# Four of the scan stage's output weight sums added by the DMA engines in place of GpSimd

## The chip, the cores and the metric

The kernel runs on one core of a Trainium2 chip. The metric is the device time in microseconds (us) of one execution; a kernel's time is the median of several runs. A profile is one further execution, recorded by the hardware profiler. Its span runs from the first to the last instruction, and its own device time is a little longer than the span.

## The reference

One layer of a diffusion backbone, in float32, over 1024 latent tokens of width 1024 and 256 context tokens ahead of them. The token mixer is a two-directional S5 state-space scan: 64 groups of 16 channels with 64 complex states each. A SwiGLU feed-forward block with 2816 hidden units follows.

```python
def s5_direction(u_ctx, u_lat, lam_re, lam_im, log_step, b_re, b_im, c_re, c_im):
    lam_bar = jnp.exp(lam * jnp.exp(log_step)[:, None])
    b_bar = ((lam_bar - 1.0) / lam)[..., None] * lax.complex(b_re, b_im)
    c_mat = lax.complex(c_re, c_im)
    def run(u, h0):
        bu = jnp.einsum('lgh,gnh->lgn', u, b_bar)
        bu = bu.at[0].add(lam_bar * h0)
        a = jnp.broadcast_to(lam_bar, bu.shape)
        _, h = lax.associative_scan(_linear_combine, (a, bu), axis=0)
        return jnp.einsum('lgn,ghn->lgh', h, c_mat).real, h[-1]
    ...
# around it: rms_norm, modulate, gelu and a gated product (GLU), then
# x + gate * swiglu(...), and a last rms_norm
```

The sums that the change touches belong to the last line of `run`: the output weights C times powers of lam_bar, one table for each of the eight token positions inside a chunk. They are complex products, so each entry is the sum of two real products.

## The kernel before

The tokens are cut into chunks of eight. A chunk's input goes into states by one set of matmuls; VectorE then runs the recurrence over the chunks, 159 of them with the context; and each chunk's outputs come from the state before it, times the output weight tables, plus a within-chunk product that acts on the inputs directly. The 64 groups are handled as four quarters q, each with two directions d. A quarter's table `CL[q]` has four parts, part = 2 ri + d (real or imaginary, forward or backward), each 128 x 1024 floats.

The order of the whole stage is written out by hand in `PROG1` (L32) and `PROG2`: a list of steps, each a letter and a number, which `run` (L945) walks through. All engines get their instructions in that order, each engine its own. The steps that matter here:

- **Cqp** (C22 is quarter 2, part 2): `cl_ops` (L660). GpSimd makes one product into the table (`prod(0, o)`), a second into a scratch tile (`prod(1, ct)`), and the two are added. The string `HOWS` (L30) has a letter for each of the sixteen sums that tells who adds: P is TensorE, E is GpSimd, Y is a transfer with accumulation that GpSimd's queue issues (L676). The first two sums of quarter 0 are issued ahead of the program with Y already, as are twelve others of an earlier stage (L434). The scratch tiles are given out by `cts` (L696): C22, C31 and C33 share one (in region `rw`), C30 and C32 another (in region `ra`).
- **Kn** (K4 and K5 are quarter 2, K6 and K7 quarter 3): `k_mats` (L806) multiplies the tables on TensorE for the within-chunk product (matmuls L813, L817, L821); ScalarE copies the result out (L825) and stores it to memory (L826).
- **Tn**: `toeplitz` (L828). SyncE loads from that memory (`ra<-kd`, L834) what the within-chunk matmul of a half quarter needs.
- **Rk**: `turned(k, 0)` (L899). ScalarE copies the backward states of half quarter k in reversed order (L906); it needs VectorE's scan of that half quarter.
- **Pk, Xk, Sk, pk**: TensorE's output matmuls of half quarter k for the first half of the chunks; `x_mm` (L936) is the within-chunk part, `states_mm` (L926) the part from states. P4 needs T8 and T9. P6 and P7 are written p6 and p7, since their `x_mm` comes in `PROG2`.
- **Yn**: ScalarE copies the result out of the accumulation banks (L988). f7 is a small piece of the scan that GpSimd does.

The end of `PROG1` reads `C22 C23 R2 X2 K4 K5 S2 Y4 Y5 R3 P3 Y6 Y7 T8 T9 T10 T11 C30 C31 R4 P4 Y8 Y9 C32 C33 f7 M2 m0 R5 P5 Y10 Y11 R6 p6 Y12 Y13 R7 K6 p7 Y14 Y15 K7 T12 ... T15`. VectorE has the scan as its own long list, which runs beside all of it; `PROG2` then does the second half of the chunks (N0 to N7), GELU and the start of the GLU.

```python
            def add():
                if how is PE:
                    ...
                elif how is SY:
                    E.dma_start(o, ct, accum_op=ADD)
                else:
                    tt(o, o, ct, ADD, E)

            o = CL[q][:, ri, d]
            return [lambda: prod(0, o), lambda: prod(1, ct), add]
...
        HOW = [[{"P": PE, "Y": SY, "E": E, "V": V}[c] for c in h] for h in HOWS.split()]
```

Of the kernel before, what the change touches and what calls it, by code (L numbers as in the profile page):

```python
# [26 lines left out]
NS = 64  # L27
EPS = 1e-6
MAGIC = 12582912.0
HOWS = "PPPP PPEE PEEE EEEE"  # L30
ZEN = "VVSVSVSV"
PROG1 = ("A22 B0 A26 C02 G1 A30 A34 C03 A40 K0 A44 A48 C10 K1 L2 A54 G2 C11 A60 F10 C12 F11 C13 T0 T1 T2 T3 A64 M0 M1 K2 K3 R0 P0 Y0 Y1 L3 R1 C20 P1 Y2 Y3 T4 "  # L32
         "T5 G3 T6 T7 C21 C22 C23 R2 X2 K4 K5 S2 Y4 Y5 R3 P3 Y6 Y7 T8 T9 T10 T11 C30 C31 R4 P4 Y8 Y9 C32 C33 f7 M2 m0 R5 P5 Y10 Y11 R6 p6 Y12 Y13 R7 K6 p7 Y14 Y15 K7 T12 T13 T14 T15")
# [10 lines left out]
def s5_ffn_kernel(tc, a, out):  # L44
# [3 lines left out]
    with ctx:  # L48
# [1040 lines left out]

        HOW = [[{"P": PE, "Y": SY, "E": E, "V": V}[c] for c in h] for h in HOWS.split()]  # L1090
        run(PROG1)
# [667 lines left out]
```

## Time and profile before

| | |
|---|---|
| median of 3 runs | 1015.07 us (1015.01 to 1017.59) |
| the profiled execution, its own time | 1015.25 us |
| its span | 1013.0 us |
| TensorE busy | 959.5 us, 95% |
| GpSimd busy | 752.3 us, 74% |
| VectorE busy | 781.8 us, 77% |

The scan stage lies at about 130 to 235 us of the span, and the steps from C22 to K7 at 182 to 231 us. In rows of the timeline, "idle before" in square brackets is the time in which that engine stood still ahead of the instruction, and behind the arrow stands what ended it. PE is TensorE's matmuls, PEld its weight loads, DVE VectorE, ACT ScalarE, POOL GpSimd, SP SyncE; a q behind a name is that engine's instruction queue. "issue" means that the profile shows nothing that was waited for.

### The profile page before, as it was taken

The numbers are of one execution on the slowest core, as the hardware profiler recorded it, in microseconds if no ns is written. First come the engines' busy times: TensorE is split into PE (matmuls) and PEld (weight loads), VectorE is DVE, ScalarE is ACT, GpSimd is POOL, SyncE is SP. The second block draws the span as 40 slices with busy tenths as digits, with TensorE's granted clock in tenths as the row PEclk, the third lists the DMA queues.
The fourth block names the chain that finished last, engine by engine and source line by source line (L and its number), as shares of the span: only waits on it lengthen the run. The fifth ranks groups of instructions, "written<-read, shape, count | busy, mean of one in ns | idle before, by whom it ended". The sixth has DMA issues, their size and how long they took to land. (4 is left out here: it accounts for less than half of the span.)

```text
span 1013.0 us, 18603 instructions
## 1 busy us (share of the span) xinstructions
PE 959.5 (95%) x6988; PEld 770.5 (76%) x6988; DVE 781.8 (77%) x1694; ACT 441.7 (44%) x862; POOL 752.3 (74%) x574
## 2 busy tenths in 40 slices
PE   5988797878999999999999999999999999999996
PEld 1466423777999988778888888888888888888885
DVE  7979799995456867877958677686958677686987
ACT  5478622335544663443343343324343343424337
POOL 5799898980872448979785878777786877777674
PEclk9999999999999999999999999999999999999998
DMA  9765996324512021011212111121212111121205
GB/s 335 280 137 97 315 332 235 93 72 142 188 47 80 1 104 63 27 44 46 73 42 83 42 52 42 49 66 52 74 42 83 43 49 46 43 72 53 73 21 166
DMA packets 48545, 98.95 MB, mean 98 GB/s; under 512 B 4284, under 2 KB 18876, under 8 KB 47176
## 3 DMA queue, kind: packets, MB, share of 16 engines
q1 hardware_dynamic: 43272, 86.64, 25.9%
q0 software_dynamic: 2016, 7.34, 3.8%
q10 hardware_dynamic: 3168, 3.79, 1.1%
q8 instruction: 55, 0.90, 0.4%
q14 instruction: 34, 0.28, 0.1%
HBM read 84.25 MB, written 6.17 MB: 89 GB/s over the span
## 5 line engine op out<-in xcount | busy, mean ns | idle before, releaser
L78 POOL TENSOR_TENSOR c<-rxc,c 128x512 fp32r<-128x512 f32 x128 | 166.6, 1316 | 53.2 <-ACT c L1213 52.4
L1273 PE MATMUL ut<-ra,c 128*128 128x512 f32 x400 | 155.7, 389 | 1.2 <-DVE ra L78 1.2
L1272 PE MATMUL ut<-ra,c 128*128 128x512 f32 x400 | 155.7, 389 | 0.2 <-ACT ra L1213 0.2
L1274 PE MATMUL ut<-ra,c 128*128 128x512 f32 x400 | 155.6, 389 | 0.0
L1213 ACT CAST c<-rxc 128x512 fp32r<-128x512 f32 x128 | 79.0, 622 | 146.5 <-PE xt L1567 53.0
L1567 PE MATMUL xt<-c,c 128*128 128x512 f32 x540 | 129.7, 389 | 0.0
L78 DVE TENSOR_TENSOR ru<-ru,xt 128x1024 f32<-128x1024 f32 x90 | 107.8, 1216 | 13.4 <-PE xt L1567 9.4
L1567 PEld LDWEIGHTS xt<-c,c 128*128 128x128 f32 x540 | 101.4, 188 | 21.0
L78 DVE TENSOR_TENSOR ru<-ut,ru 128x512 f32<-128x512 f32 x98 | 67.2, 686 | 43.0 <-PE ut L1274 37.6
L1273 PEld LDWEIGHTS ut<-ra,c 128*128 128x128 f32 x400 | 75.1, 188 | 17.1 <-POOL rxc L78 1.5
L1272 PEld LDWEIGHTS ut<-ra,c 128*128 128x128 f32 x400 | 75.1, 188 | 16.1 <-ACT ra L1213 0.6
L1274 PEld LDWEIGHTS ut<-ra,c 128*128 128x128 f32 x400 | 75.1, 188 | 15.5
L78 POOL TENSOR_TENSOR c<-rw,c 128x512 fp32r<-128x512 f32 (+1 forms) x29 | 39.8, 1372 | 37.7 <-ACT c L1213 37.7
L78 POOL TENSOR_TENSOR c<-ru,c 128x512 fp32r<-128x512 f32 (+1 forms) x39 | 58.8, 1508 | 10.1 <-ACT c L1213 5.7
L1272 PE MATMUL ut<-c,c 128*128 128x512 f32 x160 | 62.3, 390 | 0.8 <-DVE rxa L78 0.8
L78 POOL TENSOR_TENSOR rxc<-rxc 128x512 f32<-128x512 f32 x40 | 61.5, 1537 | 1.6
L1273 PE MATMUL ut<-c,c 128*128 128x512 f32 x160 | 62.3, 389 | 0.0
L1274 PE MATMUL ut<-c,c 128*128 128x512 f32 x160 | 62.2, 389 | 0.0
L1567 PE MATMUL ut<-c,c 128*128 128x512 f32 x216 | 51.9, 389 | 0.0
L78 DVE TENSOR_TENSOR pe<-pe,ru 128x256 f32<-128x256 f32 x64 | 27.4, 428 | 29.3 <-ACT pe L1113 16.2
L585 PE MATMUL pv<-ru,c 128*64 128x160 f32 x512 | 44.4, 313 | 5.7 <-ACT rxa L389 1.8
L78 DVE TENSOR_TENSOR ru<-ru,ut 128x512 f32<-128x512 f32 x76 | 47.2, 679 | 0.3
(439 smaller groups left out, 2569.5 us busy)
## 6 DMA issues: line engine op xcount, KB each, us to landing
c<-in_ada_w SPq DMA_DIRECT2D x46, 256.0 KB
rxc<-in_w SPq DMA_DIRECT2D x38, 256.0 KB
rxc<-in_w SPq DMA_DIRECT2D x19, 512.0 KB
ru<-in_w SPq DMA_DIRECT2D x11, 512.0 KB
rw<-in_w SPq DMA_DIRECT2D x11, 512.0 KB
ra<-in_ada_w SPq DMA_DIRECT2D x10, 512.0 KB
ra<-in_ada_w SPq DMA_DIRECT2D x18, 256.0 KB
ru<-in_xT SPq DMA_DIRECT2D x4, 1024.0 KB
```

What stands on the lines that cost most here:

```text
L78: eng.tensor_tensor(out=o, in0=x, in1=y, op=op)
L585: PE.matmul(pv[64 * (i % 2):64 * (i % 2) + 64, ri, c0:c0 + 160], w[:, i, 64 * ri:64 * ri + 64], U[:, 8 * b + 4 * j + i], start=True, stop= ...
L1213: S.copy(o[0], x)
L1272: PE.matmul(pu, wh, bh, start=start, stop=False)
L1273: PE.matmul(pu, wh, bl, start=False, stop=False)
L1274: PE.matmul(pu, wl, bh, start=False, stop=stop)
L1567: PE.matmul(pd, w[:, cs_], b, start=j in (1, 2, 4) and n == 0, stop=n == 2, skip_group_check=j not in (1, 2, 4))
```

## The change

Four letters of `HOWS` go from E to Y: C22, C30, C31 and C32. The sums C23 and C33 stay with GpSimd, C20 with TensorE.

```diff
-HOWS = "PPPP PPEE PEEE EEEE"
+HOWS = "PPPP PPEE PEYE YYYE"
```

On GpSimd, four tensor additions become four transfers that its queue issues. Here is its list from C30's second product on, to C33's (`c_66` is the table of quarter 3, `ra` and `rw` hold the scratch tiles, `rxc` and `rxa` the factors):

```order
 L78 TENSOR_TENSOR ra<-rxc,rxa 128x1024 [waits DMAHW5_49,DMAHW3_49,Activation_49]
-L78 TENSOR_TENSOR c_66<-c_66,ra 128x1024 [waits Pool_49]
+L676 DMA c_66<-ra 128x1024 [waits Pool_49]
 L78 TENSOR_TENSOR c_66<-rxc,rxa 128x1024
-L78 TENSOR_TENSOR rw<-rxc,rxa 128x1024
-L78 TENSOR_TENSOR c_66<-c_66,rw 128x1024 [waits Pool_49]
+L78 TENSOR_TENSOR rw<-rxc,rxa 128x1024 [waits DMASW6_49]
+L676 DMA c_66<-rw 128x1024 [waits Pool_49]
 L78 TENSOR_TENSOR c_66<-rxc,rxa 128x1024
-L78 TENSOR_TENSOR ra<-rxc,rxa 128x1024
-L78 TENSOR_TENSOR c_66<-c_66,ra 128x1024 [waits Pool_49]
+L78 TENSOR_TENSOR ra<-rxc,rxa 128x1024 [waits DMASW7_49]
```

Each addition has become a transfer in the same place, and a product that fills a scratch tile anew now waits for the transfer that read it: C31's for C22's (DMASW6), C32's for C30's (DMASW7), and likewise C33's for C31's.

On TensorE nothing moves; only waits change. In p6, the first consumer of quarter 3's table:

```order
-L926 MATMUL pw<-c_66,ra 64x128 [waits DVE_49,PE_49,Pool_49]
+L926 MATMUL pw<-c_66,ra 64x128 [waits DMASW7_49,DVE_49,PE_49]
 L926 MATMUL pw<-c_66,ra 64x128 [waits Activation_49]
-L926 MATMUL pw<-c_66,ra 64x128 [waits Activation_49,Pool_49]
+L926 MATMUL pw<-c_66,ra 64x128 [waits DMASW0_49,Activation_49]
 L926 MATMUL pw<-c_66,ra 64x128
-L926 MATMUL pw<-c_66,ra 64x128 [waits Pool_49]
+L926 MATMUL pw<-c_66,ra 64x128 [waits DMASW1_49]
 L926 MATMUL pw<-c_66,ra 64x128
 L926 MATMUL pw<-c_66,ra 64x128 [waits Pool_49]
```

The parts C30, C31 and C32 are waited for through the transfers' semaphores; the last row, for C33, still waits for GpSimd. In K4 the first matmul that reads C22 waits for its transfer, where before it had only the wait for C23, two groups of eight matmuls ahead of it:

```order
 L813 MATMUL kt<-c_65,rxa 16x112
 L813 MATMUL pm<-c_65,rxa 16x112
-L813 MATMUL kt<-c_65,rxa 16x112
+L813 MATMUL kt<-c_65,rxa 16x112 [waits DMASW6_49]
 L813 MATMUL pm<-c_65,rxa 16x112
 L813 MATMUL kt<-c_65,rxa 16x112
```

No instruction changes its place on VectorE, ScalarE or SyncE.

## Rows read from the trace of the kernel before

**Rows 1.** The page, 40 equal slices of the span: TensorE's busy tenths.
```profile
PE   5988797878999999999999999999999999999996
```
**Rows 2.** Busy time by stretch: PE, PEld, DVE, ACT, POOL, clock, DMA share, GB/s.
```profile
205.00:210.00 5.00, 2.72 (x60) 2.37 (x54) 5.00 (x30) 1.59 (x3) 4.92 (x4) 1.00 0.59 130
```
**Rows 3.** GpSimd's timeline, 120 to 260 us: start, us, engine, line, operation.
```profile
125.98 2.02 POOL L78 TENSOR_TENSOR rw<-rxc,rxa 128x1024 f32<-128x1024 f32 x1 [1.77 <-DMA c<-rw]
128.31 0.88 POOL L676 DMA_DIRECT2D c<-rw  x1 [0.30 <-POOL rw L78]
128.92 10.22 POOL L78 TENSOR_TENSOR c<-rxc,rxa 128x1024 f32<-128x1024 f32 x5
...
159.46 1.40 POOL L78 TENSOR_TENSOR c<-ra,r 128x256 f32<-128x256 f32 x2 [2.31 <-DVE ra L78]
...
183.89 2.02 POOL L78 TENSOR_TENSOR rw<-rxc,rxa 128x1024 f32<-128x1024 f32 x1
185.99 2.36 POOL L78 TENSOR_TENSOR c<-c,rw 128x1024 f32<-128x1024 f32 x1
188.30 4.03 POOL L78 TENSOR_TENSOR c<-rxc,rxa 128x1024 f32<-128x1024 f32 x2
192.41 2.35 POOL L78 TENSOR_TENSOR c<-c,c 128x1024 f32<-128x1024 f32 x1
...
218.18 2.36 POOL L78 TENSOR_TENSOR c<-c,rw 128x1024 f32<-128x1024 f32 x1
```
**Rows 4.** Accumulating transfers of L434 (twelve), then L676 (two), from issue to landing.
```profile
DMA to landing us min/median/max: 4.5/5.5/7.8
...
DMA to landing us min/median/max: 6.1/7.5/8.8
```
**Rows 5.** TensorE's timeline in K4: C23's group, and the first matmul that reads C22.
```profile
194.82 0.27 PE L813 MATMUL kt<-c,rxa 64*16 64x112 f32 x1 [1.53 <-POOL c L78]
...
195.21 0.26 PE L813 MATMUL kt<-c,rxa 64*16 64x112 f32 x1
```
**Rows 6.** TensorE's weight loads in p6.
```profile
219.90 0.36 PEld L926 LDWEIGHTS pw<-c,ra 64*64 64x64 f32 x8 [0.78 <-issue]
220.59 1.81 PEld L926 LDWEIGHTS pw<-c,ra 64*64 64x64 f32 x52 [0.33 <-POOL c L78]
```
**Rows 7.** ScalarE's timeline: R6 and R7.
```profile
219.16 0.63 ACT L906 COPY ra<-ra 128x512 f32<-128x512 f32 x1
...
224.24 0.62 ACT L906 COPY ra<-ra 128x512 f32<-128x512 f32 x1 [0.54 <-DVE ra L78]
```
**Rows 8.** VectorE's timeline: the last piece that R7 needs, and the copy behind the scan.
```profile
223.95 0.20 DVE L78 TENSOR_TENSOR ra<-ra,lta 128x64 f32<-128x64 f32 x1
...
227.30 0.43 DVE L908 COPY ra<-ra 128x512 f32<-128x512 f32 x1
```
**Rows 9.** TensorE's timeline: a stop inside K6, p7's first matmuls, N0's first.
```profile
225.27 0.19 PE L821 MATMUL kt<-rxc,rxa 64*16 64x16 f32 x1 [1.23 <-issue]
...
225.48 0.41 PE L926 MATMUL pw<-c,ra 64*64 64x128 f32 x4
...
230.48 1.22 PE L926 MATMUL pe<-c,ra 64*64 64x128 f32 x28 [0.47 <-ACT rw L825]
```
**Rows 10.** TensorE's timeline: P4's within-chunk matmuls.
```profile
208.15 1.13 PE L936 MATMUL pw<-ra,ru 128*128 128x128 f32 x8 [1.55 <-DMA ra<-kd]
```
**Rows 11.** The page's DMA queues: packets, MB, share of 16 engines' span.
```profile
q0 software_dynamic: 2016, 7.34, 3.8%
```
**Rows 12.** VectorE's timeline: starts of successive scan steps at two places.
```profile
157.31 0.28 DVE L78 TENSOR_TENSOR ltb<-ra,lta 128x128 f32<-128x128 f32 x1
158.37 0.28 DVE L78 TENSOR_TENSOR ltb<-ra,lta 128x128 f32<-128x128 f32 x1
...
193.16 0.28 DVE L78 TENSOR_TENSOR ltb<-ra,lta 128x128 f32<-128x128 f32 x1
194.21 0.28 DVE L78 TENSOR_TENSOR ltb<-ra,lta 128x128 f32<-128x128 f32 x1
```

## The prediction, written before the changed kernel was run

> **What bounds the kernel now.** I read the page's slices first: from slice 10 on, some 250 us, TensorE is busy for nine tenths or more in nearly all of them [rows 1]. A shift of what comes before is carried to the end there, and nothing in that part is touched. The change lies in the scan stage, so I read that stage alone. At 205 to 210 us GpSimd is busy for 4.92 us of 5 and VectorE for all 5, TensorE for 2.72 [rows 2]. VectorE runs the scan without a stop; GpSimd makes the weight tables without a stop; TensorE follows both. So the question is at which places TensorE waits for GpSimd, and what is late next where that wait goes.
>
> In GpSimd's timeline one sum is two products of 2.0 us and an addition of 2.36; C22's addition runs from 185.99, C23's products from 188.30 and its addition from 192.41, and the last addition, C33's, from 218.18 to 220.54 [rows 3].
>
> **What an exchanged sum saves on GpSimd.** With an addition, the next product starts 188.30 - (183.89 + 2.02) = 2.39 us behind the last product's end. With a transfer, which the trace has at 128.31, it starts 128.92 - (125.98 + 2.02) = 0.92 us behind it: the issue occupies 0.88 and the next product overlaps its end [rows 3]. So 1.47 us each, and 5.88 for the four. C23's addition then ends at 194.76 - 1.47 = 193.29. C33's would end at 220.54 - 5.88 = 214.66, less what the new waits cost.
>
> **The new waits on GpSimd.** C32's second product needs C30's transfer to have landed. Between that issue and this product lie a gap of 0.61 us, C31's two products, its issue (0.92 with its gap) and C32's first product: 0.61 + 3 x 1.98 + 0.92 = 7.5 us. The fourteen such transfers of this trace landed 4.5 to 8.8 us after issue, with medians of 5.5 and 7.5 [rows 4]; one of them made the product behind it wait for 1.77 us [rows 3]. So the wait is 0 to 1.3 us, and the same again at C33: C33's addition ends between 214.7 and 217.3. What is queued behind it on GpSimd is f7 and two small steps, and R7 is the first to need f7. Before, f7 came after 220.5; it is now at least 3 us earlier, so these waits cost nothing.
>
> **First place, K4: up to 1.47 us.** TensorE stood still for 1.53 us until C23's addition had ended, and started at 194.82 [rows 5]. That becomes 193.35. The next wait is C22's transfer. It is issued at 183.89 + 2.02 + 0.30 (the gap at 128.31) = 186.2 and lands at 190.7 to 195.0 by the bounds above. It is wanted 0.39 us after the start of C23's group (195.21 against 194.82 [rows 5]), so at 193.74. A landing of 5.5 or 7.5 us is in time; at 8.8 the gain shrinks to 195.21 - 195.0 = 0.2. I take the full 1.47, since both medians lie within the 7.5 us that are there, and keep 0.2 as the other end.
>
> K5, S2 and P3 follow on TensorE without another wait for GpSimd. P4 waits for its table of inputs (1.55 us, until 208.15 [rows 10]), but that table is loaded from what K4 and K5 stored, so it moves with them. R6 thus ends at 219.79 - 1.47 = 218.32 [rows 7].
>
> **Second place, p6: 0.33 us.** p6 began when R6 was there, loaded eight weights and then waited another 0.33 us for C33 [rows 6]. With C33 finished by 217.3 that wait is gone. Together, p6 and K6 can run 1.80 us earlier, and p7 behind them could start at 225.48 - 1.80 = 223.7 [rows 9].
>
> **What is late next: VectorE.** p7 needs R7, and R7 already waited for VectorE: 0.54 us, until the last scan piece of this half quarter at 223.95 + 0.20 [rows 7, 8]. The change moves nothing on VectorE. R7 ends at 224.24 + 0.62 = 224.86; from R6's end at 219.79 to p6's reload at 219.90 it took 0.1 us [rows 6, 7], so p7's backward matmuls start at about 225.0, where they started at 225.5 before. **Of the 1.8 us on offer, 0.5 us is left**; the rest becomes TensorE waiting for R7. Behind p7 come Y14, Y15, K7 and N0 at 230.48 [rows 9]. N0 also needs a copy that VectorE makes behind the scan, done by 227.73 [rows 8]; that is still early for an N0 at 230.0. So the 0.5 us goes on into the part that TensorE fills.
>
> The sum, against the profiled execution's own 1015.25 us (its span 1013.0 and 2.25 around it): 1015.25 - 0.5 = 1014.75. The median of the runs stands 0.18 below that execution, so I predict 1014.6 us.
>
> **Rivals.** (a) *The transfers hold up other transfers: slower.* The four additions move from GpSimd to the DMA engines, just where K4's and K5's results are stored and read back for P4. The fourteen transfers took 3.8% of 16 engines' span [rows 11]: 0.038 x 1013 / 14 = 2.75 us of all engines each. C30's is issued at about 197.6, among K5's stores, and C31's at 202.5, among the loads P4 waits for. The Trainium skill, DMA: Bandwidth & Descriptors, section "Issuing engines are not separate DMA queues", says that transfers started by the scalar, sync or gpsimd engine all end up on the same 16 DMA engines and interleave there. By that rule, what is saved on GpSimd is partly paid by whoever waits for a load. If P4's load is d late, p7 moves by the greater of -0.5 and -1.8 + d, so the point is d = 1.8. One whole transfer ahead of it, d = 2.75: +0.95, 1015.6 to 1016.2. Both, d = 5.5: +3.7, about 1018.8. Against it: in that stretch the engines are busy for 0.59 of the time [rows 2]; 2.75 us more in the 5.5 us of one landing is another 0.50, so 1.09 in all, which delays by 0.09 x 5.5 = 0.5 us, and that hides under the 1.3 us that VectorE's limit leaves.
>
> (b) *C22 lands last, and K4 gains nothing.* The transfer then does not do what it is for. p6's 0.33 us remains: 1014.9 by the profile, 1014.7 by the median. It needs a landing of about 9 us, the worst of fourteen.
>
> (c) *The stop inside K6 stays where it is.* K6 stands still for 1.23 us until 225.27, with no wait that the profile shows [rows 9]. I let it move with K6. If it belongs to the moment and not to K6, p7 still starts at 225.5 and the time stays at 1015.1.
>
> (d) *The scan itself gets faster, and VectorE's limit falls away.* This needs the additions to have slowed VectorE. One scan step took 158.37 - 157.31 = 1.06 us while GpSimd stood idle (its 2.31 us before 159.46 [rows 3]), and 194.21 - 193.16 = 1.05 during C23's addition [rows 12]. So there is nothing to win there; were there, the whole 1.8 would pass: 1013.3. The Trainium skill, SBUF — State Buffer, section "SBUF: two separate sides", states that a VectorE operation with two SBUF inputs contends with a GpSimd operation that reads SBUF. By that rule taken alone each removed addition would free VectorE; the equal steps in the trace speak against it here.
>
> **How the numbers follow.** Forecast 0.55; (a) 0.24, of which 0.08 for more than one transfer's delay; (b) 0.10; (c) 0.05; (d) 0.04; 0.02 for what I have not thought of. The range for 8 in 10 runs from (d), 1013.3, over the forecast, (b) and (c), to (a) with one transfer and something more: 1017.0. About 0.3%, 3 us, is what a measurement of this kernel can tell from no change. None of the cases is faster by that much, (a) with both delays is slower by that much: faster 0.03, same 0.87, slower 0.10.
>
> **What would show it.** Right: no wait for GpSimd at K4 and p6; GpSimd through with C33 by 217.3; R7 waiting for VectorE until the same 224.2, with R6 some 1.3 us earlier; p7 and N0 half a us earlier, and everything behind them by as much. Wrong: K4 waiting for a transfer from `rw` beyond 193.8 (b); P4's wait longer than 1.55 us and R6 later than 219.8 (a); p7 still at 225.5 although p6 ended early (c); scan steps below 1.05 us (d). A difference that arises behind N0 and not before it would be something that none of these steps has.

## The result: slower, by the transfers that wait in front of P4

The changed kernel takes 1018.02 us (median of 12 runs, 1016.38 to 1022.99) against 1014.27 us before (12 runs beside it, 1012.01 to 1017.59). The ratio is 1.0037, 95% interval 1.0026 to 1.0049: slower by 3.75 us. I had forecast 1014.6 us and given slower by over 0.3% a chance of one in ten; the time lies above the range.

What the change does to GpSimd is what I forecast. Its timeline in the changed kernel (start, us, engine, line, operation):

```profile
195.94 2.03 POOL L78 TENSOR_TENSOR ra<-rxc,rxa 128x1024 f32<-128x1024 f32 x1
198.27 0.86 POOL L676 DMA_DIRECT2D c<-ra  x1 [0.30 <-POOL ra L78]
198.88 2.32 POOL L78 TENSOR_TENSOR c<-rxc,rxa 128x1024 f32<-128x1024 f32 x1
200.87 2.31 POOL L78 TENSOR_TENSOR rw<-rxc,rxa 128x1024 f32<-128x1024 f32 x1
203.47 0.88 POOL L676 DMA_DIRECT2D c<-rw  x1 [0.30 <-POOL rw L78]
...
213.67 2.35 POOL L78 TENSOR_TENSOR c<-c,rw 128x1024 f32<-128x1024 f32 x1
```

C30's transfer is issued at 198.27 and C31's at 203.47, 5.20 us apart; a sum with an addition took 192.41 - 185.99 = 6.42 [rows 3]. GpSimd never waits for a transfer between them, and C33's addition ends at 216.02 where it ended at 220.54. TensorE no longer waits for GpSimd at K4 or in p6. The loss comes at P4. TensorE's timeline (idle time before an instruction and what ended it in brackets):

```profile
196.49 0.17 PE L821 MATMUL pm<-rxc,rxa 64*16 64x16 f32 x1 [0.81 <-issue]
199.95 0.17 PE L821 MATMUL pm<-rxc,rxa 64*16 64x16 f32 x1 [1.32 <-issue]
211.26 2.05 PE L936 MATMUL pw<-ra,ru 128*128 128x128 f32 x8 [4.15 <-DMA ra<-kd]
214.04 2.08 PE L936 MATMUL pw<-ra,ru 128*128 128x128 f32 x8 [0.73 <-DMA ra<-kd]
```

P4's second part in the kernel before, next to its first in [rows 10]:

```profile
210.12 1.16 PE L936 MATMUL pw<-ra,ru 128*128 128x128 f32 x8 [0.84 <-DMA ra<-kd]
```

Two things stand there. P4's first wait for its table was 1.55 us [rows 10] and is 4.15; and the same eight matmuls that took 1.13 us [rows 10] take 2.05. The changed kernel by stretch shows what goes with it (us, PE busy, granted clock, DMA share, GB/s):

```profile
206.00:208.00 2.00, 1.11 (x36) 1.00 0.86 136
208.00:210.00 2.00, 0.00 (x0) 1.00 0.62 151
210.00:212.00 2.00, 0.74 (x3) 0.72 1.13 187
212.00:214.00 2.00, 1.31 (x7) 0.50 0.79 138
214.00:216.00 2.00, 1.96 (x8) 0.50 0.79 196
216.00:218.00 2.00, 2.00 (x42) 0.57 0.66 183
```

TensorE does nothing from 208 to 210, and behind that its granted clock falls from 1.00 to 0.50 (2.4 to 1.2 GHz) for some 5 us. In the kernel before, the clock is 1.00 in all six of these stretches.

Why P4 waits so long is seen in two steps of its chain. K5's results are copied by ScalarE, stored, and read back as P4's table by T8. ScalarE's timeline of before, from K5's first copy to Y8:

```profile
199.74 0.36 ACT L825 COPY rw<-kt 128x240 f32<-128x240 f32 x1 [2.25 <-PE pm L821]
...
213.49 1.07 ACT L988 COPY ru<-pw 128x512 f32<-128x512 f32 x2 [5.27 <-PE pw L926]
```

and of after (its last row is R7):

```profile
200.30 0.36 ACT L825 COPY rw<-kt 128x240 f32<-128x240 f32 x1 [3.24 <-PE pm L821]
...
218.95 1.07 ACT L988 COPY ru<-pw 128x512 f32<-128x512 f32 x2 [10.23 <-PE pw L926]
...
228.53 0.63 ACT L906 COPY ra<-ra 128x512 f32<-128x512 f32 x1
```

SyncE's own timeline gives the issue of T8, which needs K5's stores to have landed; before:

```profile
203.32 4.17 SPq L834 DMA_DIRECT2D ra<-kd  x4
```

and after:

```profile
205.17 5.21 SPq L834 DMA_DIRECT2D ra<-kd  x4
```

So the stores are 4.87 us from copy to T8 where they were 3.58, because C30's transfer (issued at 198.27) is in front of them; then T8 is 6.09 us on its way where it was 4.83, because C31's (203.47) is in front of that. The DMA queues of the changed kernel from 206 to 208 us, one to three us after T8's issue (packets, MB, share of the 16 engines; q0 holds the accumulating transfers, q1 the table loads):

```profile
q0 software_dynamic: 74, 0.27, 86.1%
q1 hardware_dynamic: 2, 0.00, 0.2%
```

and from 208 to 210:

```profile
q1 hardware_dynamic: 564, 0.28, 59.1%
...
q0 software_dynamic: 8, 0.00, 0.4%
```

The load gets 2 packets while the transfer runs and 564 once it is through. In the kernel before, the load's first packets come 1.3 us after T8's issue; here they come 2.7 us after it, when the transfer is nearly through. This load does not share with the transfer; it stands behind it.

Put together, from the copy of half quarter 1's outputs just ahead of K4 (L988, at 190.48 before and 191.62 after) to N0 (230.48 [rows 9] and 235.20):

| step | before | after | change |
|---|---|---|---|
| to K5's first copy | 9.26 | 8.68 | -0.58 |
| K5's copy to T8's issue | 3.58 | 4.87 | +1.29 |
| T8's issue to P4's first matmul | 4.83 | 6.09 | +1.26 |
| P4's first part to its second | 1.97 | 2.78 | +0.81 |
| second part to Y8's copy | 3.37 | 4.91 | +1.54 |
| Y8's copy to N0 | 16.99 | 16.25 | -0.74 |
| sum | 40.00 | 43.58 | +3.58 |

The hold-up of stores and load is 2.55 us, the two steps with the low clock 2.35, and what the change was to bring 1.32. The two executions differ by 1.14 us ahead of this stretch, and before has a drop of the clock of its own behind N0, at 242 to 248 us, which after has not; I put neither down to the change. So the own times of the two executions, 1017.96 and 1015.25 us, differ by 2.71 only. The sum of 3.58 comes near the 3.75 of the medians, but that is in part luck: where and how often the clock falls varies from execution to execution, as the profiles below show.

### The profile page after: what moved, and what is told of

It is laid out like the page before. It is cut to its first block, busy times and chain, and to the rows that moved or that the text cites. A ratio compares the mean times of both kernels' runs of the same rounds, so it can differ in the third digit from the quotient of the medians.

```text
span 1016.1 us, 18610 instructions
## 1 busy us (share of the span) xinstructions
PE 959.4 (94%) x6988; PEld 771.7 (76%) x6988; DVE 782.1 (77%) x1694; ACT 441.5 (43%) x862; POOL 747.0 (74%) x574
## 5 line engine op out<-in xcount | busy, mean ns | idle before, releaser
L78 POOL TENSOR_TENSOR c<-rxc,rxa 128x1024 f32<-128x1024 f32 x23 | 48.0, 2168 | 0.1
```

The costliest lines, as they stand in the source:

```text
L78: eng.tensor_tensor(out=o, in0=x, in1=y, op=op)
```

## Experiments

The sums are chosen by one table of letters, four rows of four for the quarters: `Y` is a transfer, `E` GpSimd's addition, `N`, `M` and `X` what the experiment puts there. Theory A: the transfers stand in front of K5's stores and P4's load, TensorE pauses and its clock falls. Theory B: it is the earlier end of GpSimd's sums that costs. Theory C: any of the transfers costs, or the loss lies elsewhere. Ratios are to the kernel before on the same chip, with 95% intervals. A profile is one execution and need not be a typical one: that of C22 with C32 took 1010.95 us beside a median of 1014.71, that of the changed kernel without P4's dependence 1022.38 beside 1014.94.

**The early release without the transfers.** The four sums are left out, so GpSimd is as early, or earlier, and no transfer runs:

```
-HOWS = "PPPP PPEE PEEE EEEE"
+HOWS = "PPPP PPEE PENE NNNE"
...
+                elif how is None:
+                    pass
```

> The four sums C22, C30, C31 and C32 are left out altogether: neither GpSimd nor a transfer adds the second product, so GpSimd is through even earlier and the DMA engines get no more work than before. Theory A (the transfers hold up the stores and loads between K4, K5 and P4, and TensorE then waits): without transfers the harm is gone; P4 waits for its load no longer than the 1.55 us of before, R7 waits for VectorE, and the time is 0.3 to 0.6 us under the kernel before. Theory B (GpSimd's early release itself disturbs TensorE: K4 and K5 start without a pause and then stop without a visible cause, 0.81 and 1.32 us in the changed kernel): these stops stay, and the time stays 2 us or more above the kernel before.

Measured: 1014.19 us, ratio 0.9996 (0.9971 to 1.0020). P4 waits once, 0.44 us:

```profile
210.09 1.16 PE L938 MATMUL pw<-ra,ru 128*128 128x128 f32 x8 [0.44 <-DMA ra<-kd]
```

B wanted 2 us or more, and the interval ends at 2.0; the stops in K4 and K5 are there (0.53 and 1.50 us) without the loss. So an early GpSimd alone does not make it, and B falls. But it also brings nothing that can be told: with all the time of the four additions given back, the kernel is level with before, and the 0.5 us that I had forecast lies within the interval. What becomes of the time is seen at R7, which waits for VectorE longer than the 0.54 us of before [rows 7]:

```profile
224.49 0.62 ACT L908 COPY ra<-ra 128x512 f32<-128x512 f32 x1 [1.25 <-DVE ra L78]
```

**One transfer at a time.** C22, C30 and C31, each alone:

```
-HOWS = "PPPP PPEE PEEE EEEE"
+HOWS = "PPPP PPEE PEYE EEEE"
...
+HOWS = "PPPP PPEE PEEE YEEE"
...
+HOWS = "PPPP PPEE PEEE EYEE"
```

> Only C22 goes to a transfer. Theory A: its transfer, issued near 186 us, lies beside the loads T6 and T7, which nobody needs soon; K4 starts earlier, P4's load moves with it and waits for no transfer: 0 to 0.6 us under the kernel before. Theory B: K4 starts early in this kernel too, so the stops in K4 and K5 come, and the time is 1 us or more above the kernel before.

> Only C30 goes to a transfer, issued near 199 us, beside the stores of K4 and K5. Theory A: the stores land later, T8 is issued later, P4's wait grows by 0.5 to 2 us, and the time by 0 to 1.5 us. Theory B: K4 still waits for C23 as before, so nothing changes: within 0.5 us of the kernel before.

> Only C31 goes to a transfer, issued near 205 us, beside the load T8 that P4 waits for. Theory A: this is the costliest of the four; T8 lands 2 to 3 us later, TensorE's clock falls after the longer pause, and the time is 1 to 3.5 us above the kernel before. Theory B: K4 as before, within 0.5 us of the kernel before.

Measured: C22 alone 0.9996 (0.9976 to 1.0015), C30 alone 1.0013 (0.9995 to 1.0032), C31 alone 1.0016 (0.9992 to 1.0040). By these intervals no single one can be told from no change. They are wide, though: by the medians C30 alone is 1.5 us above before (1016.69 against 1015.20) and C31 alone 3.1 us (1018.29), nearly the whole loss. How the loss divides between the two stays open. With C30's transfer, T8 is issued 6.39 us behind K5's copy (200.61 to 207.00); with C31's alone that step is 3.82, and P4's second part waits for its load. C30 alone, then C31 alone:

```profile
211.86 3.86 PE L936 MATMUL pw<-ra,ru 128*128 128x128 f32 x16 [3.05 <-DMA ra<-kd]
```

```profile
210.78 1.13 PE L936 MATMUL pw<-ra,ru 128*128 128x128 f32 x8 [1.48 <-DMA ra<-kd]
214.72 2.07 PE L936 MATMUL pw<-ra,ru 128*128 128x128 f32 x8 [2.81 <-DMA ra<-kd]
```

C31 alone is not quite the case of the changed kernel: its transfer is issued at 206.02, 1.08 us behind T8 and not ahead of it. The two then run side by side. From 208 to 210 the table loads have 320 packets and the transfer 41. From 212 to 214 each has 47, and since the transfer's are some ten times larger (0.19 MB against 0.02), the load hardly moves:

```profile
q0 software_dynamic: 47, 0.19, 48.0%
q1 hardware_dynamic: 47, 0.02, 5.7%
```

A warning belongs here: the one profile of C22 alone also has P4 wait 3.71 us and the clock at 0.50 behind it, with no transfer beside the load, while its 12 runs are level with before. Its load starts in time, with first packets 1.3 us after T8's issue; why the rest takes longer stays open. One trace of a wait of this kind is not proof; the next pairs are.

**The two that lie in the chain, and the two that don't.**

```
-HOWS = "PPPP PPEE PEEE EEEE"
+HOWS = "PPPP PPEE PEEE YYEE"
...
+HOWS = "PPPP PPEE PEYE EEYE"
```

> Only the sums C30 and C31 are made by transfers; C22 and C32 stay GpSimd additions. Theory A (the two transfers C30 and C31 lie in front of K5's stores and of P4's table load, TensorE then stops for about 4 us at P4 and its granted clock falls): as the whole change, 2 to 4 us slower than before, P4's two waits over 3.5 us together, clock 0.5 to 0.6 for 4 to 6 us behind them. Theory C (the loss needs all four, or is no one pair's): within 1 us of before.

> Only C22 and C32 by transfers: C22's is issued ahead of K4's stores and some 10 us ahead of P4's load, C32's behind that load. Theory A: no loss, 0 to 0.6 us faster than before (K4's wait for GpSimd is 1.2 us shorter and the stops take part of that back). Theory C (any two transfers cost half of the whole): 1.5 to 2 us slower.

Measured: C30 and C31 1018.04 us, ratio 1.0036 (1.0021 to 1.0052); C22 and C32 1014.71 us, ratio 1.0006 (0.9987 to 1.0024). These two transfers carry the whole loss, and with the other two none shows: it is their place that costs, not their number. TensorE's P4 with C30 and C31 (the clock there stayed at 1.00; of my expectation the waits were near but short of it, 3.25 us in all, and the drop was not there in this execution, which had one to 0.50 at 202 to 204):

```profile
211.99 1.13 PE L936 MATMUL pw<-ra,ru 128*128 128x128 f32 x8 [2.48 <-DMA ra<-kd]
213.88 1.16 PE L936 MATMUL pw<-ra,ru 128*128 128x128 f32 x8 [0.77 <-DMA ra<-kd]
```

and with C22 and C32, where it waits once:

```profile
210.52 1.16 PE L936 MATMUL pw<-ra,ru 128*128 128x128 f32 x8 [0.47 <-DMA ra<-kd]
```

**The transfers without the change.** All additions stay on GpSimd; C30 and C31 get an extra transfer of the same size into an area that nobody reads:

```
-HOWS = "PPPP PPEE PEEE EEEE"
+HOWS = "PPPP PPEE PEEE XXEE"
...
+                elif how is S:
+                    E.dma_start(view(RA, 8, [8, T, HC]), ct, accum_op=ADD)
+                    tt(o, o, ct, ADD, E)
```

> All four additions stay on GpSimd, and nothing waits for a transfer; for C30 and C31 one extra accumulating transfer of 0.5 MB into a dead area is issued just ahead of the addition. Theory A: the transfers alone cost 1 to 3 us (GpSimd is 0.6 us later per issue besides, which is on the path at K4 at most once). Theory B (the loss comes from when GpSimd's sums end): at most 1 us.

Measured: 1019.44 us, ratio 1.0056 (1.0039 to 1.0073), 4.7 us by the medians and more than the 1 to 3 that I expected. P4 waits 4.40 us, and the clock follows:

```profile
211.08 1.13 PE L939 MATMUL pw<-ra,ru 128*128 128x128 f32 x8 [1.94 <-DMA ra<-kd]
214.67 2.08 PE L939 MATMUL pw<-ra,ru 128*128 128x128 f32 x8 [2.46 <-DMA ra<-kd]
```

```profile
214.00:216.00 2.00, 1.33 (x6) 0.50 0.58 168
216.00:218.00 2.00, 2.00 (x28) 0.50 0.32 96
```

I had forgotten that GpSimd is slowed as well: behind such an issue its addition takes 2.66 us instead of 2.36, so C33 ends at 222.34 and TensorE waits another 0.78 us for the small steps that GpSimd does behind it. Part of the 4.7 us is thus likely GpSimd's. Nor is it the whole chain of the changed kernel: C30's extra transfer, issued 3.56 us ahead of K5's copy, is out of the way of its stores (3.47 us from copy to T8), and C31's is issued 0.49 us behind T8, so that it meets P4's second part, as with C31 alone. What the run shows is that transfers in this stretch cost time though no sum ends earlier and nothing waits for them.

**Is it the accumulation or the bytes?** The four transfers copy instead of adding, so the first product is left out of the four sums:

```
-HOWS = "PPPP PPEE PEEE EEEE"
+HOWS = "PPPP PPEE PEME MMME"
...
+                elif how is S:
+                    E.dma_start(o, ct)
```

> The four transfers stay, with the same size, queue and place, but they copy instead of accumulating: the first product is left out of the four sums. If it is the bytes in the 16 engines that hold up K5's stores and P4's load, this is as slow as the change (2 to 4 us above before). If it is the accumulation (read, add and write back), the transfers land earlier than 4.9 to 9.6 us and the time is within 1 us of before, or below it.

Measured: 1017.75 us, ratio 1.0028 (1.0013 to 1.0044). Without the addition C30's transfer lands 3.5 us after its issue instead of 4.9 and C31's 5.0 instead of 5.2, and the loss is nearly the same. So it is mostly that half a megabyte is in front, not that it is added. In this execution the loss took another form: P4 waits 2.16 us, but TensorE stops for 5.5 us within K4 and K5 (waits from 190 to 216 us: total, times, longest):

```profile
PE pm L823 <- issue: 5.5, 2, 2.8
PE pw L938 <- DMA ra<-kd: 2.2, 2, 1.5
```

**Take P4 out of the chain.** T8 and T9 read a table stored long before, in both kernels; P4's part of the result comes from the wrong table:

```
-            rows = KD_[q][32 * gi:32 * gi + HC]
+            rows = KD_[1 if u in (8, 9) else q][32 * gi:32 * gi + HC]
```

> The kernel before, but P4's two table loads T8 and T9 read the table that is stored earlier (of the half before), so that they need not wait for K5's stores; P4's part of the result is computed from the wrong table. Both theories: P4's waits of 1.55 and 0.84 us go, so 1 to 2.5 us below before.

> The changed kernel with the same edit of T8 and T9, so that neither K5's stores nor these loads can be late for P4, whatever the transfers do to them. Theory A (the loss is the chain K5's stores, T8, P4, and the lower clock behind its pause): the change costs nothing here, within 1 us of the other kernel with this edit, and 1 to 2.5 us below before. Theory C (the transfers cost TensorE, GpSimd or the end something elsewhere): it stays 2 us or more above the other kernel with this edit.

Measured: before with this edit 1014.29 us, ratio 0.9996 (0.9978 to 1.0014); the changed kernel with it 1014.94 us, ratio 0.9999 (0.9981 to 1.0017). With all four transfers running, the loss does not show as soon as P4 does not hang on K5's stores and T8: the interval ends at 1.7 us above before, where the change stands 3.75 above. That speaks for A and against C. My number for both was a miss: in the kernel before, 2.4 us of waits at P4 went and nothing was won. That agrees with the step of the prediction that has R7 next: in this run R7 waits 0.39 us for one of GpSimd's small steps, where it waited for VectorE before, and not for TensorE:

```profile
224.60 0.62 ACT L906 COPY ra<-ra 128x512 f32<-128x512 f32 x1 [0.39 <-POOL r L78]
```

The profile of the changed kernel with the edit has stops of 3.8 us in K4 and K5, but it is of the slowest of its 12 executions, 1022.38 us, and can't show that such stops are free. What speaks for small ones costing little are the sums left out and C22 with C32: stops of 2.0 and 2.2 us in K4 and K5, in executions of 1012.96 and 1010.95 us.

**The two kernels once more.**

> A second look at the kernel before: P4's two waits together 1 to 3 us, no drop of the granted clock between 208 and 218 us, if the first look was typical.

> A second look at the changed kernel: theory A wants P4's two waits together at 4 us or more again and a granted clock of 0.5 to 0.7 for some us behind them, or, if that pattern is one execution's, the copies of K5 to the issue of T8 again over 4.5 us against 3.6 before.

Before: P4 waits 0.28 + 0.66 us, less than the first time and than I expected. After: 3.00 + 0.66 us at P4, the clock at 0.50 behind it, and 5.42 us from K5's copy (205.37) to T8's issue:

```profile
199.90 0.17 PE L821 MATMUL pm<-rxc,rxa 64*16 64x16 f32 x1 [2.98 <-issue]
205.00 0.18 PE L821 MATMUL pm<-rxc,rxa 64*16 64x16 f32 x1 [2.96 <-issue]
216.62 1.13 PE L936 MATMUL pw<-ra,ru 128*128 128x128 f32 x8 [3.00 <-DMA ra<-kd]
218.40 1.57 PE L936 MATMUL pw<-ra,ru 128*128 128x128 f32 x8 [0.66 <-DMA ra<-kd]
```

K5 is so late here that everything stands behind the next transfer: its stores behind C31's (issued at 203.50), and T8, issued at 210.79, behind C32's (208.71). From 210 to 212 the queue of the transfers had

```profile
q0 software_dynamic: 96, 0.39, 100.9%
```

with not one packet of the table load; its first came at 213.1, 2.3 us after T8's issue. That execution took 1022.62 us; it has the stops in K4 and K5 of the plain copies on top. No version here beats the kernel before: C22 and C32 alone are level with it.

## Why the prediction was wrong, step by step

- **What a sum saves on GpSimd: 1.47 us each, nearly right.** The gap behind the issue is as forecast, 0.91 us; but the two products behind it take from 198.88 to 203.18, 4.30 us where two took 4.03 [rows 3], so 1.22 us are saved. C33 ended at 216.02, within 214.7 to 217.3, and the new waits cost nothing.
- **K4: mis-sized.** I took 1.47 us; K5's copy came 0.58 earlier relative to the work ahead of K4. The 1.53 us wait for C23 [rows 5] is gone, but TensorE now stops for 0.81 + 1.32 us within K4 and K5 with no wait that the profile shows, where before it stopped for 0.33. C22 landed in time, so rival (b) did not come.
- **"That table is loaded from what K4 and K5 stored, so it moves with them": the step that failed.** K5's stores landed and T8's load arrived later in their chain by 1.29 and 1.26 us. I had the mechanism as rival (a), with both transfers at about 1018.8 us, and the two places were right: C30's in front of K5's stores, C31's in front of the load. What I did wrong was to dismiss it by an average: a DMA share of 0.59 plus 0.50 for the transfer, 1.09, so 0.5 us of delay. That takes the stretch as one pool in which everything shares. The share in front of K5's stores was even lower, 0.23 from 200 to 202 us in the kernel before, and they were held up as long. The trace has 2 packets of the load in 2 us and 564 in the next two. For a load that is issued 1.7 us behind a transfer of half a megabyte, the price is the transfer's remaining run, not the excess of the mean over 1. By the same rows the bound was 0 to 2.75 us for each, and both places lie in one chain, so they add. (The low end that I gave for one transfer, 1015.6 us, is a slip too: 0.95 us above the 1015.07 of before is 1016.0.)
- **The clock was not in the sum at all.** A longer wait at P4 was priced as its own length. In the profile shown the granted clock stood at 0.50 behind TensorE's pause, and P4's two steps took 2.35 us more. That is not all a loss against before: its profile has a drop of its own behind N0, and executions that lose nothing have one too, to 0.50 from 200 to 202 us with the sums left out (1012.96 us) and with C22 and C32 (1010.95 us). With C30 and C31 alone the clock fell at 202 to 204 instead, and the time was the same as the change's. So a drop at P4 is not needed for the loss, and what it adds on average stays open.
- **p6 was right, and R7 where the loss is away.** The wait for C33 is gone; from Y8 to N0 the changed kernel is 0.74 us shorter. R7 comes so late there that it waits for nothing, so VectorE's limit was not met. It is seen in the kernels without the loss: R7 waits for VectorE 1.25 us with the sums left out and 0.97 with C22 and C32, until 224.49 and 224.62, where it waited 0.54 until 224.24 [rows 7]. That this limit keeps most of any gain fits that these two, and before with P4 taken out of the chain, are level with before.
- **(c) was not decided:** K6's stop was 0.46 us instead of 1.23, but p7 stands behind R7, which is late. **(d) did not come:** from 182 to 222 us a scan step takes 1.05 us in both kernels, and also with the sums left out.

The Trainium skill, DMA: Bandwidth & Descriptors, section "Issuing engines are not separate DMA queues", which I had cited for (a), says that transfers of all engines run on the same 16 and interleave. The first half is what these runs show. The second is what they show where the transfer is issued behind the load, 47 packets of each with C31 alone; the load issued behind the transfer saw little of it, 2 packets against 74.

## What to carry to other kernels

A transfer that replaces an engine's work is not free where that engine is not the limit: look for the stores and loads that someone waits for while it lands (here 4.9 to 9.6 us), and price what is issued behind it as waiting for all that is left of the transfer, not for a share of the mean. Leaving the work out altogether is the cheapest first experiment: here it would have shown, before any transfer was placed, that there was too little to win to be measured. And behind a longer wait of TensorE, look at the granted clock before the wait is priced as its own length.

## What the runs showed of the hardware

**A transfer goes ahead of what is issued behind it.** One accumulating transfer of half a megabyte held 16 engines at 86 to 101% of a 2 us stretch. A table load issued 1.7 and 2.1 us behind such a transfer had its first packets 2.7 and 2.3 us after its issue, where it was 1.3 in both profiles of the kernel before. K5's stores show it best. Five profiles have a transfer issued 0.8 to 2.0 us ahead of K5's copy (the changed kernel twice, C30 alone, C30 with C31, the plain copies): from the copy to T8 it takes 4.87 to 6.39 us. Six have none there (before twice, the sums left out, C22 alone, C31 alone, C22 with C32): 3.36 to 3.92 us. The other way round, with the transfer issued behind the load, both run at once, as with C31 alone above.

**Stops of TensorE with no wait in the profile.** In K4 and K5, where it issues hundreds of short matmuls, TensorE stops for 0.3 to 3.0 us. The DMA view has packets of a queue called instruction. In the changed kernel, one of these falls at 193.8 to 194.0 us:

```profile
q8 instruction: 1, 0.02, 42.1%
```

and the next at 197.6 to 197.8:

```profile
q8 instruction: 1, 0.02, 29.8%
```

The stops end at 196.49 and 199.95, so 2.7 and 2.4 us behind the start of these 0.2 us. Over the fourteen profiles of the kernels above there are 22 such stops of 0.27 us and more; the distance is 2.3 to 2.9 us in all but one, which has 3.4. Not every packet has a stop behind it: C30 alone has the packets and none. Before, the first of these packets comes at 192.6, 2.2 us ahead of the start of C23's group at 194.82 [rows 5], so the wait for C23 may have covered most of what the packet would have cost. In the other execution of the changed kernel the packet came at 197.4, at the end of a table load that C22's transfer had held up (from 190 to 194 us 40 packets of it beside 97 of the transfer), and the stop was 2.98 us, until 199.90. The Trainium skill, Runtime: NRT & Kernel Launch, section "Instruction fetch mechanics", states that instructions come in blocks of 16 KiB over a DMA queue of the sequencer's own, mostly hidden. The packets of 0.02 MB fit that, and so would a K4 that gains little from an earlier GpSimd, if its instructions come no earlier. If the fetch causes the stops, "mostly hidden" does not hold in this stretch. That is the likely reading; no run here separates it.

**GpSimd behind the issue of a transfer.** The two operations of 128 x 1024 behind the issue take about 2.3 us each instead of 2.03, and 2.66 instead of 2.36 for an addition; their starts stay 2.0 us apart, so a pair of products ends 0.3 us later. It is not the running transfer alone that slows them: C33's addition in the changed kernel, 5 us behind the issue of C32, took 2.35 us, though from 213.6 to 216.1 that transfer still had 40 packets.
